# The state products of an S5 branch on unsplit float32 operands

## The chip, the cores and the metric

The kernel runs on one core of one Trainium2 chip. Five engines work side by side and meet only through semaphores: TensorE multiplies matrices (PE; its weight loads are listed as PEld), VectorE (DVE), ScalarE (ACT) and GpSimd (POOL) work on tiles in SBUF and PSUM, and SyncE (SP) issues nearly all DMAs. The metric is the device time of one execution in microseconds.

## The reference, cut to what matters

One layer of a hybrid encoder over 4096 tokens of width 1024: a norm, one combined projection, three branches side by side, an output projection, a second norm and the residual. The branch at issue is the state space model (SSM). Its 256 channels form 16 groups of 16 channels, each with 64 complex states per direction:

```python
bu = einsum('blgp,gnp->blgn', u, bb)                      # inputs into states (re, im)
h  = associative_scan(complex_linear_combine, lam, bu)    # forward and reverse
y  = einsum('blgn,gpn->blgp', h_re, c_re) - einsum('blgn,gpn->blgp', h_im, c_im)
```

The last line, the product of the states with C, is what is changed.

## The kernel before, in words

All products that need float32's precision are made from split parts: ScalarE rounds an operand to float32r (`hi`), VectorE or GpSimd subtracts that from the operand (`lo`), and TensorE makes three float32r products, hi·hi, hi·lo and lo·hi, into one PSUM bank (`mm3`, L989 to L992, is such a triple).

TensorE's order is written out by hand: `Slots` (L84) is a clock that advances by one slot after every 6 matmuls of the running projection (`chunk`, L354), and every helper step is booked into a slot with `e.at`. An engine's queue therefore holds its instructions in slot order, and waits stand in front of the instruction that needs them. The program has four stages: projections with weights and norm (stage 1), attention (stage 2), the gates' projections (stage 3, 24 slots for each of 8 blocks of 512 tokens, lines L1129 to L1155), and the output projection `w_out` (L1278).

The SSM runs inside stage 3, one group every 8 slots (`SSM_PACE`, L76), so three or four groups are under way at a time. A group's 512 columns hold 8 tokens each. Its steps, by the slot within the group (L1103 to L1109):

- 0: SP loads the group's record `rec` (weights, C, angles; 689 columns) and its inputs `u`.
- 3 to 7: splits of the record's input weights (`wb`) and of `u` (`ur`, its low part on POOL); the angles `ang` on POOL; ACT makes cosines and sines `cs` (slots 8 to 10).
- 11, 12: TensorE makes the inputs of the states, `vr` and `vi`, and the direct term, which opens the group's bank `y`.
- 12 to 14: DVE and POOL turn the inputs by the angles (tiles `wt` and `t`). Slot 14 also splits C into `wc` (L1064, L1065): ACT rounds it, DVE makes the low part one slot later.
- 15, 16: four DVE scans over half the partitions each (L1069, L1071) write `gs`.
- 18 to 23: the states are turned back: `back_cos` on DVE (wt<-gs,cs), `back_sin` on POOL (gs<-gs,cs), two sums on POOL (wt<-wt,gs).
- 25 to 27: the states are split into tiles `h`: ACT rounds, DVE makes two low parts (`state_lo`, L1088).
- 29, 30: six matmuls (y<-h,wc) add C times the states to `y`; 31: ACT copies `y` out; 33: SP stores it.

Of two groups' work in DVE's queue, the one that stands behind `back_cos` of a group is `state_lo` of the group before it, then the turning of the next. At the end of stage 3, `load_wo` (L1115) loads the output weights through three buffers (`rawo`), and DVE makes their low parts (`wo`).

Of the kernel before, what the change touches and what calls it, by code (L numbers as in the profile page):

```python
# [11 lines left out]
F32R = mybir.dt.float32r  # L12
# [4 lines left out]
P = 128  # L17
# [8 lines left out]
NC = SEQ // L  # L26
# [9 lines left out]
REC = 689  # L36
# [93 lines left out]
def hybrid_kernel(ctx, tc, A, out):  # L130
    nc = tc.nc
    V, S, PL, T = nc.vector, nc.scalar, nc.gpsimd, nc.tensor
    dma = nc.sync.dma_start
# [4 lines left out]
    swd = tc.dram_tile([G, P, REC], F32, name="swd")  # L138
# [22 lines left out]
    def tt(eng, out, in0, in1, op):  # L161
        return eng.tensor_tensor(out=out, in0=in0, in1=in1, op=op)  # L162
# [9 lines left out]
    def copy(out, in_):  # L172
        return S.activation(out=out, in_=in_, func=AF.Copy)  # L173

    def bank(i, shape, nm):
        return banks[i].tile(shape, F32, tag="b", name=nm)

    def bc(ap, shape):
        return ap.to_broadcast(shape)

    def f(ap):
        return ap.bitcast(F32)

    def lo_part(lo, src, hi, eng):
        tt(eng, lo, src, f(hi), ALU.subtract)

    def split(hi, lo, src, eng, lag=1, scale=None):

        copy(hi, src)
        if lag:  # L190
            e.at(e.now + lag, lo_part, lo, src, hi, eng)
        else:
            lo_part(lo, src, hi, eng)
# [795 lines left out]
    def mm3(o, wh, wl, r, first, last):  # L989
        T.matmul(o, lhsT=wh, rhs=r[:, 0], start=first, stop=False)  # L990
        T.matmul(o, lhsT=wh, rhs=r[:, 1], start=False, stop=False)
        T.matmul(o, lhsT=wl, rhs=r[:, 0], start=False, stop=last)  # L992

    def ssm_group(g, R, t0):


        sv = R["sv"]
        rho = bc(R["rho"][:, g:g + 1], [P, NC])
        X = {}

        def new(nm, shape, dt=F32, bufs=1):
            X[nm] = sv.tile(shape, dt, tag=nm, name=nm, bufs=bufs)
            return X[nm]

        def load():
            dma(out=new("rec", [P, REC], bufs=2), in_=swd[g])
            dma(out=new("u", [P, NC], bufs=2), in_=udram[g].rearrange("q s c -> s q c"))

        def inputs_hi():
            copy(new("ur", [P, 2, NC], F32R, 2)[:, 0], X["u"])  # L1010
            copy(new("wb", [P, 2, 3, P], F32R, 2)[:, 0], X["rec"][:, 0:384].rearrange("p (m c) -> p m c", m=3))

        def wb_lo():
            w = X["wb"]
            lo_part(w[:, 1], X["rec"][:, 0:384].rearrange("p (m c) -> p m c", m=3), w[:, 0], V)

        def turns():
            shc = [P, 16, 32]  # L1020
            rec = X["rec"]
            tt(PL, new("ang", shc), bc(rec[:, 672:688].unsqueeze(2), shc), bc(rec[:, 640:672].unsqueeze(1), shc),
               ALU.add)

        def ur_lo():
            lo_part(X["ur"][:, 1], X["u"], X["ur"][:, 0], PL)

        def angle_abs():
            cs = new("cs", [P, 2, NC], bufs=2)
            av = X["ang"].rearrange("p a b -> p (a b)")  # L1030
            S.activation(out=cs[:, 0], in_=av, func=AF.Abs)
            S.activation(out=cs[:, 1], in_=av, func=AF.Abs, bias=cst[:, C_NQ:C_NQ + 1])

        def angle_fold():
            S.activation(out=X["cs"], in_=X["cs"], func=AF.Abs, bias=cst[:, C_NHALF:C_NHALF + 1])

        def angle_sin():
            S.activation(out=X["cs"], in_=X["cs"], func=AF.Sin, scale=-TURN, bias=cst[:, C_HPI:C_HPI + 1])

        def inputs_mm():  # L1040
            w, ur = X["wb"], X["ur"]
            for i, nm in enumerate(("vr", "vi")):
                X[nm] = bank(4 + i, [P, NC], nm)
                mm3(X[nm], w[:, 0, i], w[:, 1, i], ur, True, True)

        def direct_mm():
            w = X["wb"]
            X["o"] = bank((6, 7, 2, 3)[g % 4], [P, NC], "y")
            mm3(X["o"], w[:, 0, 2], w[:, 1, 2], X["ur"], True, False)

        def turn_re():
            wt, t2 = new("wt", [P, 2, NC], bufs=2), new("t2", [P, 2, NC])
            tt(V, wt[:, 0], X["vr"], X["cs"][:, 0], ALU.mult)
            tt(V, t2[:, 0], X["vi"], X["cs"][:, 1], ALU.mult)

        def turn_im():
            wt, t2 = X["wt"], X["t2"]
            tt(PL, wt[:, 0], wt[:, 0], t2[:, 0], ALU.add)
            tt(V, wt[:, 1], X["vi"], X["cs"][:, 0], ALU.mult)
            tt(V, t2[:, 1], X["vr"], X["cs"][:, 1], ALU.mult)  # L1060

        def turn_sum():
            tt(PL, X["wt"][:, 1], X["wt"][:, 1], X["t2"][:, 1], ALU.subtract)
            wc = new("wc", [P, 2, 2, P], F32R, 2)  # L1064
            split(wc[:, 0], wc[:, 1], X["rec"][:, 384:640].rearrange("p (m c) -> p m c", m=2), V)  # L1065

        def scan(i):
            gs, wt = R["gs"][g % 2], X["wt"]
            V.tensor_tensor_scan(out=gs[0:64, i, 1:NC], data0=rho[0:64, 0:NC - 1], data1=wt[0:64, i, 0:NC - 1],  # L1069
                                 initial=0.0, op0=ALU.mult, op1=ALU.add)  # L1070
            V.tensor_tensor_scan(out=gs[64:128, i, NC - 2::-1], data0=rho[64:128, 0:NC - 1],  # L1071
                                 data1=wt[64:128, i, NC - 1:0:-1], initial=0.0, op0=ALU.mult, op1=ALU.add)

        sh2 = [P, 2, NC]

        def back_cos():
            tt(V, X["wt"], R["gs"][g % 2], bc(X["cs"][:, 0].unsqueeze(1), sh2), ALU.mult)

        def back_sin():
            tt(PL, R["gs"][g % 2], R["gs"][g % 2], bc(X["cs"][:, 1].unsqueeze(1), sh2), ALU.mult)  # L1080

        def back_sum(i):
            tt(PL, X["wt"][:, i], X["wt"][:, i], R["gs"][g % 2][:, 1 - i], ALU.add if i else ALU.subtract)

        def state_hi(i):
            copy(new(f"h{i}", [P, 2, NC], F32R)[:, 0], X["wt"][:, i])

        def state_lo():  # L1088
            for i in range(2):
                h = X[f"h{i}"]  # L1090
                lo_part(h[:, 1], X["wt"][:, i], h[:, 0], V)

        def state_mm(i):
            wc = X["wc"]
            mm3(X["o"], wc[:, 0, i], wc[:, 1, i], X[f"h{i}"], False, i == 1)

        def out_copy():
            copy(new("yg", [P, NC], bufs=2), X["o"])

        def store():  # L1100
            dma(out=ybuf[g].rearrange("q s c -> s q c"), in_=X["yg"])

        for t, fn, a in ((0, load, ()), (3, inputs_hi, ()), (4, wb_lo, ()), (6, turns, ()), (7, ur_lo, ()),  # L1103
                         (8, angle_abs, ()), (9, angle_fold, ()), (10, angle_sin, ()), (11, inputs_mm, ()),
                         (12, direct_mm, ()), (12, turn_re, ()), (13, turn_im, ()), (14, turn_sum, ()),
                         (15, scan, (0,)), (16, scan, (1,)), (18, back_cos, ()), (19, back_sin, ()),
                         (22, back_sum, (0,)), (23, back_sum, (1,)), (25, state_hi, (0,)), (26, state_hi, (1,)),
                         (27, state_lo, ()), (29, state_mm, (0,)), (30, state_mm, (1,)), (31, out_copy, ()),
                         (33, store, ())):  # L1109
            e.at(t0 + t, fn, *a, label="ssm")  # L1110

    WO = {}
# [284 lines left out]
    def to_p3():  # L1397
        e.settle("p2")
        R2["ph"].close()
        R3.update(p3_open())  # L1400
        for g in range(G):
            ssm_group(g, R3, e.now + int(SSM_PACE * g))
# [115 lines left out]
```

## Time and profile before

| | |
|---|---|
| median of three runs | 1667.59 us (1665.9 to 1668.29) |
| profiled execution | 1664.75 us, its span 1663.0 us |
| PE busy | 1574.8 us, 95% of the span |
| DVE busy | 1152.4 us, 69% |
| ACT busy | 766.5 us, 46% |
| POOL busy | 665.0 us, 40% |
| mean granted TensorE clock | 0.98 of full speed |
| SSM stretch | about 930 to 1250 us of the span |

Busy shares are averages over stages with different limits. A matmul's recorded length is that of one instruction in a pipeline, so neighbours overlap, and the distance from one start to the next is what a matmul costs. L162 is the line of a helper through which every two-operand instruction is recorded, so those are told apart by their tiles. A square bracket behind an instruction holds the engine's idle time ahead of it and what ended it.

### The profile page before, as it was taken

What the parts mean: (1) busy time and instruction counts of PE and PEld (TensorE: products, weight loads), DVE (VectorE), ACT (ScalarE), POOL (GpSimd) and SP (SyncE); (2) the same over time, 40 slices, a digit from 0 to 9 for tenths busy, and PEclk for the clock granted to TensorE, in tenths of its full rate; (3) what the DMA queues carried; (4) which work ended last, traced back from release to release, by engine and by line L of the source; (5) the groups of instructions that cost most, each with busy time, mean ns of one, the idle gap of its engine ahead of it and who ended that gap; (6) DMA issues with size and microseconds to landing.
All of it is one profiled execution on the core that took longest, in us unless ns stands there. A gap on an engine that the chain in (4) does not pass through costs nothing.

```text
span 1663.0 us, 20965 instructions
## 1 busy us (share of the span) xinstructions
PE 1574.8 (95%) x7364; PEld 1296.1 (78%) x7364; DVE 1152.4 (69%) x2047; ACT 766.5 (46%) x1624; POOL 665.0 (40%) x382
## 2 busy tenths in 40 slices
PE   8999899999999999999999989888879999999998
PEld 6787678888888888888888777676667788888886
DVE  5764676437777777777877399999985665555451
ACT  5424333346666666666776343433433333323221
POOL 0322122203233333233332277777752555555542
PEclk8999999999999999999999999999989999999999
DMA  6598999861111312123322655454635545555542
GB/s 227 174 301 262 285 302 309 290 237 63 64 64 64 118 66 71 64 75 116 133 89 89 209 182 169 121 176 144 207 122 183 188 156 176 176 179 179 176 152 76
DMA packets 131694, 267.60 MB, mean 161 GB/s; under 512 B 32386, under 2 KB 65922, under 8 KB 119812
## 3 DMA queue, kind: packets, MB, share of 16 engines
q1 hardware_dynamic: 126020, 251.57, 46.6%
q10 hardware_dynamic: 5568, 14.68, 2.6%
q8 instruction: 58, 0.95, 0.2%
q14 instruction: 48, 0.39, 0.1%
HBM read 173.25 MB, written 94.01 MB: 161 GB/s over the span
## 4 chain that ended last, share of the span: by engine, by line
PE 57%; DVE 22%; DMA 11%; issue 4%; POOL 4%; ACT 2%; SPq 1%; ACTq 0%; DVEq 0%; POOLq 0%
PE mm L350 7%; PE mm L351 7%; PE mm L352 7%; PE po L848 5%; DMA xs<-in_x_dram 5%; PE tp L858 5%; PE o L1289 5%; PE o L1287 5%; PE o L1288 5%; DVE gs L1069 4%; DVE gs L1071 4%; PE mm L361 4%; DVE h L162 3%; PE s L819 3%; PE s L818 3%
## 5 line engine op out<-in xcount | busy, mean ns | idle before, releaser
L350 PE MATMUL mm<-xk,w 128*128 128x512 f32 x968 | 388.3, 401 | 1.2 <-ACT xk L268 1.2
L351 PE MATMUL mm<-xk,w 128*128 128x512 f32 x968 | 383.5, 396 | 0.0
L352 PE MATMUL mm<-xk,w 128*128 128x512 f32 x968 | 382.1, 395 | 0.8 <-DVE w L162 0.8
L162 POOL TENSOR_TENSOR ns<-ns,es 128x1536 f32<-128x1536 f32 (+1 forms) x64 | 172.5, 2695 | 410.2 <-ACT pp L173 186.4
L352 PEld LDWEIGHTS mm<-xk,w 128*128 128x128 f32 x968 | 184.3, 190 | 41.9 <-DVE w L162 1.6
L350 PEld LDWEIGHTS mm<-xk,w 128*128 128x128 f32 x968 | 185.0, 191 | 36.6 <-ACT xk L268 1.9
L351 PEld LDWEIGHTS mm<-xk,w 128*128 128x128 f32 x968 | 184.7, 191 | 34.7 <-DVE xk L165 1.0
L820 DVE CUSTOM_DVE_ANT_0 ns<-s,cst,nsink 128x384 f32<-128x384 f32 (+1 forms) x256 | 145.7, 606 | 84.8 <-PE s L819 84.1
L1287 PE MATMUL o<-wo,yk 128*128 128x512 f32 x512 | 201.1, 393 | 3.0 <-ACT gg L1147 2.6
L1289 PE MATMUL o<-wo,yk 128*128 128x512 f32 x512 | 200.9, 392 | 2.1 <-DVE yk L165 2.1
L1288 PE MATMUL o<-wo,yk 128*128 128x512 f32 x512 | 200.4, 391 | 0.0
L173 ACT ACTIVATE pp<-tp 128x512 fp32r<-128x512 f32 x188 | 112.3, 597 | 170.6 <-PE tp L858 169.8
L361 PE MATMUL mm<-xk,w 128*128 128x512 f32 x552 | 149.3, 410 | 14.4 <-DVE xk L162 5.4
L809 ACT ACTIVATE ns<-ns,nm 128x384 f32<-128x384 f32 (+1 forms) x256 | 152.3, 598 | 2.0 <-DVE nm L820 2.0
L162 DVE TENSOR_TENSOR pp<-tp,pp 128x512 fp32r<-128x512 f32 x188 | 129.1, 687 | 18.8 <-ACT pp L173 17.4
L361 PEld LDWEIGHTS mm<-xk,w 128*128 128x128 f32 x552 | 103.3, 194 | 43.5 <-ACT xk L173 8.1
L848 PE MATMUL po<-pp,vr 128*128 128x512 f32 x376 | 127.8, 421 | 0.0
L162 POOL TENSOR_TENSOR xk<-xt,xk 128x512 fp32r<-128x512 f32 x32 | 51.8, 1625 | 172.8 <-ACT xk L173 111.0
L858 PEld LDWEIGHTS tp<-cst,ns 128*128 128x128 f32 x752 | 93.0, 140 | 34.6 <-issue 10.1
L858 PE MATMUL tp<-cst,ns 128*128 128x128 f32 x752 | 112.7, 272 | 7.3 <-DVE pp L162 7.3
L1287 PEld LDWEIGHTS o<-wo,yk 128*128 128x128 f32 x512 | 96.9, 189 | 24.4 <-ACT gg L1147 3.0
L1289 PEld LDWEIGHTS o<-wo,yk 128*128 128x128 f32 x512 | 96.9, 189 | 23.1 <-DVE yk L165 2.6
(293 smaller groups left out, 2795.3 us busy)
## 6 DMA issues: line engine op xcount, KB each, us to landing
xk<-xd SPq DMA_DIRECT2D x60, 1024.0 KB
xd<-xk SPq DMA_DIRECT2D x32, 1024.0 KB
xt<-in_xT_dram SPq DMA_DIRECT2D x35, 512.0 KB
xres<-in_x_dram SPq DMA_DIRECT2D x32, 512.0 KB
out_dram<-ot SPq DMA_DIRECT2D x31, 512.0 KB
xs<-in_x_dram ACTq DMA_DIRECT2D x24, 512.0 KB
raw<-in_w_in_dram SPq DMA_DIRECT2D x32, 256.0 KB
yattn<-ysb SPq DMA_DIRECT2D x32, 256.0 KB
```

The costliest lines, as they stand in the source:

```text
L162: return eng.tensor_tensor(out=out, in0=in0, in1=in1, op=op)
L350: T.matmul(o, lhsT=w[:, 0, k], rhs=xh, start=(k == 0), stop=False)
L351: T.matmul(o, lhsT=w[:, 0, k], rhs=xl, start=False, stop=False)
L352: T.matmul(o, lhsT=w[:, 1, k], rhs=xh, start=False, stop=(k == NK - 1))
L361: T.matmul(o, lhsT=w[:, i, k], rhs=XK[b, k][h], start=(n == 0), stop=(n == 3 * NK - 1))
L809: S.activation(out=ns[:, hh, :nk], in_=ns[:, hh, :nk], func=AF.Exp, scale=-1.0, bias=nm[:, hh:hh + 1], accum_out=su[:, hh:hh + 1])
L820: V.tensor_tensor_reduce(out=ns[:, hh, :nk], in0=sp_[:, :nk], in1=cst[:, C_D + c0:C_D + c0 + nk], scale=-(2.0 ** -(h + 1)), scalar=R["nsin ...
L848: T.matmul(po, lhsT=VR[:, (ta + kb) % 8, kv], rhs=pp[:, i], start=(kb == 0 and i == 0), stop=(kb == nkb - 1 and i == 1))
L858: T.transpose(tp[:, hh], ns[:, hh, kb * P:(kb + 1) * P], ident)
L1287: T.matmul(o, lhsT=y[:, 0, ts_], rhs=WO[kk][:, 0, hs], start=first, stop=False)
L1288: T.matmul(o, lhsT=y[:, 0, ts_], rhs=WO[kk][:, 1, hs], start=False, stop=False)
L1289: T.matmul(o, lhsT=y[:, 1, ts_], rhs=WO[kk][:, 0, hs], start=False, stop=last)
```

## The change

The six matmuls of a group's state products become two on float32 operands, straight from the record and from `wt`. The rounding and the low parts of `wc` and `h` go, with their tiles; the record, which is now read until the state products, gets four buffers instead of two; the products move from slots 29 and 30 to 26 and 27, the copy from 31 to 28 and the store from 33 to 30.

```diff
         def load():
-            dma(out=new("rec", [P, REC], bufs=2), in_=swd[g])
+            dma(out=new("rec", [P, REC], bufs=4), in_=swd[g])
             dma(out=new("u", [P, NC], bufs=2), in_=udram[g].rearrange("q s c -> s q c"))
...
         def turn_sum():
             tt(PL, X["wt"][:, 1], X["wt"][:, 1], X["t2"][:, 1], ALU.subtract)
-            wc = new("wc", [P, 2, 2, P], F32R, 2)
-            split(wc[:, 0], wc[:, 1], X["rec"][:, 384:640].rearrange("p (m c) -> p m c", m=2), V)
...
-        def state_hi(i):
-            copy(new(f"h{i}", [P, 2, NC], F32R)[:, 0], X["wt"][:, i])
-
-        def state_lo():
-            for i in range(2):
-                h = X[f"h{i}"]
-                lo_part(h[:, 1], X["wt"][:, i], h[:, 0], V)
-
         def state_mm(i):
-            wc = X["wc"]
-            mm3(X["o"], wc[:, 0, i], wc[:, 1, i], X[f"h{i}"], False, i == 1)
+            T.matmul(X["o"], lhsT=X["rec"][:, 384 + 128 * i:512 + 128 * i], rhs=X["wt"][:, i], start=False,
+                     stop=(i == 1))
...
-                         (22, back_sum, (0,)), (23, back_sum, (1,)), (25, state_hi, (0,)), (26, state_hi, (1,)),
-                         (27, state_lo, ()), (29, state_mm, (0,)), (30, state_mm, (1,)), (31, out_copy, ()),
-                         (33, store, ())):
+                         (22, back_sum, (0,)), (23, back_sum, (1,)), (26, state_mm, (0,)), (27, state_mm, (1,)),
+                         (28, out_copy, ()), (30, store, ())):
```

Lines behind the change have smaller numbers in the changed kernel: the scans L1069 and L1071 are L1067 and L1069 there, and the state products are L1084.

On VectorE, one group's round in the middle of the stretch, from one `back_cos` to the last scan ahead of the next, before:

```order
L162 TENSOR_TENSOR wt<-gs_8795,cs 128x1024
L162 TENSOR_TENSOR h_9226<-wt,h_9226 128x512
L162 TENSOR_TENSOR h_9237<-wt,h_9237 128x512
L162 TENSOR_TENSOR wt<-vr,cs 128x512
L162 TENSOR_TENSOR t_9275<-vi,cs 128x512
L162 TENSOR_TENSOR wb<-rec,wb 128x384
L162 TENSOR_TENSOR wt<-vi,cs 128x512
L162 TENSOR_TENSOR t_9275<-vr,cs 128x512
L1069 SCALAR_TENSOR_TENSOR gs_8798<-rho,wt 64x511
L1071 SCALAR_TENSOR_TENSOR gs_8798<-rho,wt 64x511
L162 TENSOR_TENSOR wc<-rec,wc 128x256
L1069 SCALAR_TENSOR_TENSOR gs_8798<-rho,wt 64x511
```

and in the changed kernel:

```order
L162 TENSOR_TENSOR wt<-gs_8795,cs 128x1024
L162 TENSOR_TENSOR wt<-vr,cs 128x512
L162 TENSOR_TENSOR t_9254<-vi,cs 128x512
L162 TENSOR_TENSOR wb<-rec,wb 128x384
L162 TENSOR_TENSOR wt<-vi,cs 128x512
L162 TENSOR_TENSOR t_9254<-vr,cs 128x512
L1067 SCALAR_TENSOR_TENSOR gs_8798<-rho,wt 64x511
L1069 SCALAR_TENSOR_TENSOR gs_8798<-rho,wt 64x511
L1067 SCALAR_TENSOR_TENSOR gs_8798<-rho,wt 64x511
L1069 SCALAR_TENSOR_TENSOR gs_8798<-rho,wt 64x511
```

Two `h` instructions and one `wc` instruction are gone, and the rest stands in the order it had. POOL's order is the same in both kernels.

On TensorE, where a block's first chunk (mm<-xk,w) meets a group's products, before:

```order
L361 MATMUL mm<-xk,w 128x512 x12
L990 MATMUL vr<-ur,wb 128x512
L991 MATMUL vr<-ur,wb 128x512
L992 MATMUL vr<-ur,wb 128x512
L990 MATMUL vi<-ur,wb 128x512
L991 MATMUL vi<-ur,wb 128x512
L992 MATMUL vi<-ur,wb 128x512
L361 MATMUL mm<-xk,w 128x512 x6
L990 MATMUL y<-ur,wb 128x512
L991 MATMUL y<-ur,wb 128x512
L992 MATMUL y<-ur,wb 128x512
L361 MATMUL mm<-xk,w 128x512 x6
```

and in the changed kernel:

```order
L361 MATMUL mm<-xk,w 128x512 x6
L1084 MATMUL y<-wt,rec 128x512
L361 MATMUL mm<-xk,w 128x512 x6
L1084 MATMUL y<-wt,rec 128x512
L990 MATMUL vr<-ur,wb 128x512
L991 MATMUL vr<-ur,wb 128x512
L992 MATMUL vr<-ur,wb 128x512
L990 MATMUL vi<-ur,wb 128x512
L991 MATMUL vi<-ur,wb 128x512
L992 MATMUL vi<-ur,wb 128x512
L361 MATMUL mm<-xk,w 128x512 x6
L990 MATMUL y<-ur,wb 128x512
```

The state products of a group now stand ahead of the `vr` of the group two after it; before, they stood a few slots behind that.

On VectorE at the end of the stretch, from the last group's `back_cos` on, before:

```order
L162 TENSOR_TENSOR wt<-gs_8798,cs 128x1024
L162 TENSOR_TENSOR h_10809<-wt,h_10809 128x512
L162 TENSOR_TENSOR h_10824<-wt,h_10824 128x512
L162 TENSOR_TENSOR wo<-rawo,wo 128x512
L162 TENSOR_TENSOR yk<-pgl,yk 128x1024
L162 TENSOR_TENSOR wo<-rawo,wo 128x512 x3
L162 TENSOR_TENSOR h_10914<-wt,h_10914 128x512
L162 TENSOR_TENSOR h_10925<-wt,h_10925 128x512
```

and in the changed kernel:

```order
L162 TENSOR_TENSOR wt<-gs_8798,cs 128x1024
L162 TENSOR_TENSOR wo<-rawo,wo 128x512
L162 TENSOR_TENSOR yk<-pgl,yk 128x1024
L162 TENSOR_TENSOR wo<-rawo,wo 128x512 x5
L162 TENSOR_TENSOR yk<-ya,yk 128x1024
```

The first low part of the output weights follows `back_cos` at once; before, two `h` instructions stood between them.

## Rows read from the trace of the kernel before

**Rows 1.** The page's first line.

```profile
span 1663.0 us, 20965 instructions
```

**Rows 2.** The chain of waits, one round: start us, us, what.

```profile
1045.17 3.40 DVE h L162 x2
...
1056.15 1.09 DVE wc L162
...
1061.66 1.23 DVE wt L162
```

**Rows 3.** Busy time by rounds: us, busy (instructions) by engine, clock, DMA, GB/s.

```profile
1007.45:1025.20 17.75, 17.48 (x64) 13.81 (x64) 17.52 (x14) 7.33 (x13) 13.21 (x7) 0.83 0.46 145
...
1096.02:1113.73 17.71, 14.71 (x63) 11.75 (x63) 17.48 (x14) 7.27 (x13) 13.17 (x7) 1.00 0.24 73
...
sum 230.31, PE 202.13 PEld 160.26 DVE 227.38 ACT 94.74 POOL 171.41; mean PE 15.55 PEld 12.33 DVE 17.49 ACT 7.29 POOL 13.19
```

**Rows 4.** Who waited for whom, 960 to 1203: total us, times, longest.

```profile
PE vr L991 <- POOL ur L162: 30.2, 14, 3.6
```

**Rows 5.** Timeline of DVE, the first rounds: start us, us, instruction.

```profile
957.81 1.22 DVE L162 TENSOR_TENSOR wt<-gs,cs 128x1024 f32<-128x1024 f32 x1
...
960.40 1.53 DVE L162 TENSOR_TENSOR wb<-rec,wb 128x384 fp32r<-128x384 f32 x1 [0.17 <-ACT wb L173]
...
967.60 1.10 DVE L162 TENSOR_TENSOR wc<-rec,wc 128x256 fp32r<-128x256 f32 x1
968.62 2.28 DVE L1069 TENSOR_TENSOR_SCAN gs<-rho,wt 64x511 f32<-64x511 f32 x1
...
973.09 1.23 DVE L162 TENSOR_TENSOR wt<-gs,cs 128x1024 f32<-128x1024 f32 x1
```

**Rows 6.** Timeline of POOL beside it.

```profile
959.11 2.41 POOL L162 TENSOR_TENSOR gs<-gs,cs 128x1024 f32<-128x1024 f32 x1 [4.25 <-DVE wt L162]
...
966.45 1.96 POOL L162 TENSOR_TENSOR ang<-rec 128x512 f32<-128x512 f32 x1
968.37 1.45 POOL L162 TENSOR_TENSOR wt<-wt,gs 128x512 f32<-128x512 f32 x1
969.78 2.19 POOL L162 TENSOR_TENSOR ur<-u,ur 128x512 fp32r<-128x512 f32 x1
```

**Rows 7.** Timeline of PE, one round at full clock.

```profile
1096.02 0.50 PE L991 MATMUL vr<-ur,wb 128*128 128x512 f32 x1 [1.44 <-POOL ur L162]
...
1110.33 0.40 PE L990 MATMUL vr<-ur,wb 128*128 128x512 f32 x1
1113.73 0.50 PE L991 MATMUL vr<-ur,wb 128*128 128x512 f32 x1 [3.00 <-POOL ur L162]
```

**Rows 8.** Float32 products of stage 1: all of a line, then two in the timeline.

```profile
L659 PE MATMUL kp<-obr,bz 128*64 128x128 f32 x32 | 6.9, 299 | 0.4 <-DVE obr L162 0.4
...
282.03 0.38 PE L659 MATMUL kp<-obr,bz 128*64 128x128 f32 x2
282.25 0.38 PE L661 MATMUL kp<-obi,bz 128*64 128x128 f32 x2
```

**Rows 9.** Timeline of DVE at the end of the stretch.

```profile
1205.22 4.34 DVE L162 TENSOR_TENSOR h<-wt,h 128x512 fp32r<-128x512 f32 x2
...
1222.03 1.33 DVE L162 TENSOR_TENSOR wc<-rec,wc 128x256 fp32r<-128x256 f32 x1
1223.28 1.21 DVE L1069 TENSOR_TENSOR_SCAN gs<-rho,wt 64x511 f32<-64x511 f32 x1
...
1228.95 3.47 DVE L162 TENSOR_TENSOR h<-wt,h 128x512 fp32r<-128x512 f32 x2
1232.35 1.77 DVE L162 TENSOR_TENSOR wo<-rawo,wo 128x512 fp32r<-128x512 f32 x1
```

**Rows 10.** Timeline of PE, its two longest pauses after that.

```profile
1229.69 0.80 PE L991 MATMUL y<-h,wc 128*128 128x512 f32 x1 [9.57 <-DVE h L162]
...
1254.79 0.50 PE L1287 MATMUL o<-wo,yk 128*128 128x512 f32 x1 [2.57 <-ACT gg L1147]
```

## The prediction, on record before the changed kernel was run

> **What bounds the kernel now.** I read the chain of waits first. From 960 to 1203 us it holds hardly anything but VectorE: scans, the two low parts of `h` (3.40 us), the low part of `wc` (1.09 us), then `back_cos` (wt<-gs,cs) of the next group, and round again [rows 2]. The table of rounds comes next. Between one `vr` wait and the next lie 17.71 to 17.75 us, 13 rounds take 230.31 us, so 17.72 us each, and DVE is busy for 17.49 of them: it is the bound [rows 3]. TensorE is not. In a round at full clock it has 14.71 us of work [rows 3] and then stands still until POOL has made the low part of `ur`: 3.00 us in the round shown, 30.2 us in 14 waits [rows 4, 7]. So TensorE follows this stretch at DVE's pace, although it is 95% busy over the span, and what shortens DVE's round shortens the program down to the next limit.
>
> **What goes.** From DVE, per group, the pair of `h` and `wc`. Start to start, `wc` takes 968.62 - 967.60 = 1.02 us [rows 5], and the pair is 3.40 us of the chain [rows 2]: 4.4 us of 17.72. From ACT go three copies per group; it is busy for 7.29 us of a round [rows 3], so that counts for nothing.
>
> **What the round comes down to.** DVE's own sum would be 17.7 - 4.4 = 13.3 us. POOL stands in the way: `back_cos` is followed by `back_sin` (gs<-gs,cs) on POOL, POOL then makes the sums that the scans wait for, and DVE and POOL slow each other. `wb` lasts 1.53 us and ends at 961.93, just after `back_sin` has ended at 959.11 + 2.41 = 961.52 [rows 5, 6]. The trace holds one round that already lacks the pair: the low parts of the first group stand behind `back_cos` at 973.09, so the round from `back_cos` at 957.81 to that at 973.09 has none [rows 5]. It takes 15.28 us, and only `wc` is in it that the changed kernel lacks. How much of that goes? At least the time in which `wc` alone runs: POOL's `ang` ends at 966.45 + 1.96 = 968.41 and `wc` at 967.60 + 1.10 = 968.70, so 0.29 us; POOL's instructions from 966.45 to 969.78 + 2.19 = 971.97 stand end to end and stay [rows 5, 6]. At most its 1.02 us. The new round is thus 14.3 to 15.0 us. I take 15.0, since POOL's row of instructions does not get shorter by `wc`'s going.
>
> This is where a rule of the Trainium skill speaks against a larger gain: "SBUF — State Buffer", section "Who interferes with whom", has VectorE (with two SBUF inputs) and GpSimd take one shared port pair as an exclusive lock, for a whole instruction, with the other fully blocked. By it the two engines' instructions add up instead of overlapping, and the gap that `wc` leaves is filled by the next of POOL's: 15.0 rather than 14.3. The `wb` that ends 0.41 us behind `back_sin` agrees.
>
> **What TensorE needs.** From 1096.02 to 1110.33, and 0.23 for the last, 14.54 us hold 63 matmuls [rows 3, 7]: 0.231 us each. Six go: 57 x 0.231 = 13.15 us. Two float32 products of 512 columns come, and no row shows one. The nearest: 16 float32 products of 128 columns (L659, four for each of four batches) have 32 records, so a product is two, and two products start 282.25 - 282.03 = 0.22 us apart [rows 8]. Four times the columns can take four times as long at most, 0.88 us; at least two matmuls' pace, 0.46 us. TensorE's round is then 13.15 + 2 x 0.46 = 14.1 to 13.15 + 2 x 0.88 = 14.9 us. The three products that one replaces took 0.69, so TensorE may gain or lose. I take 0.88, since streaming 512 columns is what these rows scale with, and 14.9 is still under 15.0: its cover is thin, 0.1 us of each round.
>
> "FP8 and Floating Point Precision", section "TensorE Precision Notes", in the Trainium skill has true float32 take four passes. By it a product would be 4 x 0.231 = 0.92 us, the round 15.0, and the cover nothing.
>
> **Waits that are added.** The products now wait for POOL's sums themselves, where ACT and DVE stood between, and behind them in TensorE's queue stand `vr` and all of the projection. But the second sum ends at 969.82, and `ur`, for which `vr` waits anyway, at 971.97 [rows 6]: 2.15 us later, while product and first `vr` take 0.88 + 0.23. So no new pause. The record's next load waited for `wc`; with four buffers it waits for state products of four groups earlier, long past. POOL's queue is unchanged, SP's store comes earlier.
>
> **Before and after these rounds.** Group 0's `wc` stands alone on DVE ahead of 957.81: 1.0 us. The round 957.81 to 973.09 gives 15.28 - 15.0 = 0.3. At the end, between the last rounds and the first low part of the output weights (`wo`, 1232.35), go a pair of 4.34 us, a `wc` of 1223.28 - 1222.03 = 1.25 us and a pair of 1232.35 - 1228.95 = 3.40 us [rows 9]. POOL's instructions fill part of the pairs' place, so 1.25 to 9.0 us; I take the middle, 5. Loads of output weights wait for `wo`'s buffers, and on them `w_out` at 1254.79. TensorE gets there in time: its pause of 9.57 us for `h` goes or shrinks [rows 10], and its pause ahead of `w_out` stays. All behind that is as before.
>
> **Sum.** 13 x (17.72 - 15.0) = 35.4, and 1.0 + 0.3 + 5 = 6.3: 41.7 us. The profiled execution took 1664.75 us (span 1663.0 [rows 1]); less 41.7 that is 1623. The median of the runs shown is 2.8 us above the profiled one, so 1626 us.
>
> **Rivals.**
>
> 1. DVE and POOL overlap more than I grant; the round is 14.3, with TensorE's products near 0.46. 13 x 3.42 = 44.5, 1.0 + 1.0, and 9 at the end: 55 us, so 1612. For it: bounds from rows, above. Against it: `wb`'s wait.
>
> 2. TensorE becomes the bound through its clock. In the round from 1007.45 the granted clock is 0.83 of 2.4 GHz, so part of it at 1.2 GHz, after a wait for `ur`, and TensorE's work is 17.48 instead of 14.71 us [rows 3]. In 13 rounds TensorE is busy for 202.13 us, 13 x 14.71 = 191.2 at full clock, so 10.9 us went to the lower level, hidden in TensorE's pauses. If that stays, a round needs 14.9 + 0.84 = 15.7: 13 x 2.0 + 6.3 = 32 us, so 1635. Against it: such a drop stands behind pauses of TensorE, and those nearly vanish.
>
> 3. A product of 512 columns costs more than four of 128, 1.7 us say (each record twice my upper value). Round 13.15 + 3.4 = 16.6: 13 x 1.1 + 6.3 = 21, so 1646. For it: no row of that shape. Against it: rows 8.
>
> 4. The stretch keeps its pace: something beside DVE holds it at 17.7, as a load that arrives late. Only the end's 1 to 5 us go: 1664. Against it: DVE is busy for all but 0.2 us of a round [rows 3].
>
> 5. Slower: the lower clock takes hold of the stretch. TensorE needs 14.9 us a round at full clock, so it exceeds today's 17.72 once the mean clock is below 14.9 / 17.72 = 0.84. At 0.75 a round is 19.9 us: 13 x 2.2 - 6 = 22 more, so 1690. For it: 0.83 has been seen in one round. Against it: in that round TensorE had waited for POOL, and here it is to be busy throughout.
>
> **How the numbers follow.** Forecast 60% (its own range 1617 to 1634), rival 1 12%, rival 2 13%, rival 3 7%, rival 4 4%, rival 5 4%. The range 1610 to 1642 takes in the first two rivals and leaves out the others, some 15%. No change within 0.2% (3.3 us, about what a measurement of this kernel tells from none) is rival 4; faster is the rest but rival 5: 92%, 4%, 4%.
>
> **What would show it.** Right: in the rounds, `back_cos` to `back_cos` of 15.0 us; DVE idle for about a microsecond per round at the scans, waiting for POOL; POOL with hardly an idle stretch; four PE records per group on L1084, starting some 0.44 us apart; the `vr` wait under half a microsecond and the clock at 1.00; `wo` and `w_out` some 42 us earlier. Wrong: rounds of 15.5 us or more with PE without a pause (product or clock); rounds of 14.5 or less; a pause on L1084 itself for POOL's sums; or rounds at 15 and `w_out` less than 35 us earlier, which would mean that a load at the stretch's end takes the gain back.

## The result and the profile after

The changed kernel takes 1623.91 us (median of four runs, 1621.85 to 1628.71), the kernel before on the same chip 1666.74 us (four runs, 1664.34 to 1668.29). The ratio is 0.9746, with a 95% interval of 0.9723 to 0.9769. The profiled execution of the changed kernel, 1628.71 us, is the slowest of its four, and that of before, 1664.75 us, is 2.0 us under its median; the two profiles therefore show a difference of 36.0 us where the medians show 42.8.

The first line of the page answers to [rows 1]:

```profile
span 1626.8 us, 20824 instructions
```

The table by windows answers to [rows 3]. Its columns are the stretch, its length, the busy time (instructions) of PE, PEld, DVE, ACT and POOL, the granted clock, the DMA share and GB/s. The rows are the first round (from `back_cos` to `back_cos`) and the thirteen behind it:

```profile
960.74:974.63 13.89, 13.28 (x55) 9.89 (x54) 13.82 (x11) 5.33 (x9) 12.59 (x7) 1.00 0.70 234
974.63:1167.21 192.58, 191.79 (x792) 147.64 (x791) 185.71 (x130) 79.06 (x118) 176.99 (x92) 1.00 0.59 193
```

192.58 / 13 = 14.81 us a round, where it was 17.72. TensorE is now busy for all but 0.79 us of the thirteen rounds, and its clock is at 1.00. The waits in this stretch answer to [rows 4]; the columns are total us, number and longest:

```profile
PE vr L991 <- POOL ur L162: 0.8, 1, 0.8
...
POOL gs L162 <- DVE wt L162: 15.1, 13, 1.2
```

TensorE's wait for the low part of `ur` has all but gone: 0.8 us in place of 30.2. The wait that remains is POOL's, 1.16 us in each round, until DVE has finished `back_cos`.

One round of DVE (its four products out of PSUM left out), and then POOL beside it, answer to [rows 5, 6]. The columns are start, us, instruction and, in brackets, idle time before it with what ended it:

```profile
1137.64 2.12 DVE L162 TENSOR_TENSOR wt<-gs,cs 128x1024 f32<-128x1024 f32 x1
...
1140.89 1.78 DVE L162 TENSOR_TENSOR wb<-rec,wb 128x384 fp32r<-128x384 f32 x1
...
1143.87 2.29 DVE L1067 TENSOR_TENSOR_SCAN gs<-rho,wt 64x511 f32<-64x511 f32 x1
1146.17 2.16 DVE L1069 TENSOR_TENSOR_SCAN gs<-rho,wt 64x511 f32<-64x511 f32 x1
1148.34 1.91 DVE L1067 TENSOR_TENSOR_SCAN gs<-rho,wt 64x511 f32<-64x511 f32 x1
1150.26 2.15 DVE L1069 TENSOR_TENSOR_SCAN gs<-rho,wt 64x511 f32<-64x511 f32 x1
1152.44 2.12 DVE L162 TENSOR_TENSOR wt<-gs,cs 128x1024 f32<-128x1024 f32 x1
```

```profile
1136.49 2.19 POOL L162 TENSOR_TENSOR ur<-u,ur 128x512 fp32r<-128x512 f32 x1
1139.84 2.41 POOL L162 TENSOR_TENSOR gs<-gs,cs 128x1024 f32<-128x1024 f32 x1 [1.16 <-DVE wt L162]
1142.20 1.63 POOL L162 TENSOR_TENSOR wt<-wt,t 128x512 f32<-128x512 f32 x1
1143.79 1.29 POOL L162 TENSOR_TENSOR wt<-wt,gs 128x512 f32<-128x512 f32 x1
1145.04 2.20 POOL L162 TENSOR_TENSOR wt<-wt,t 128x512 f32<-128x512 f32 x1
1147.21 1.96 POOL L162 TENSOR_TENSOR ang<-rec 128x512 f32<-128x512 f32 x1
1149.13 2.19 POOL L162 TENSOR_TENSOR wt<-wt,gs 128x512 f32<-128x512 f32 x1
1151.29 2.19 POOL L162 TENSOR_TENSOR ur<-u,ur 128x512 fp32r<-128x512 f32 x1
```

In this round DVE shows no idle time, but it does wait. `back_cos`, 1.22 us in [rows 5], now lasts 2.12: POOL's `ur` ends at 1138.68, a microsecond into it. `back_cos` then ends at 1139.76, and POOL's `back_sin` begins at 1139.84. A wait between these two engines stands inside the duration of the instruction that waits, on POOL too: its sums of 128x512 last 1.29 to 2.20 us in this one round. POOL's records stand end to end but for one idle stretch: 13.61 us busy and 1.16 us of waiting make the round.

Read by their ends, these lines are one row. After `back_cos` (1139.76) end `back_sin` at 1142.25 and `wb` at 1142.67; then two sums of POOL, then scan, sum, scan, `ang`, scan, sum, scan, `ur` and `back_cos`, each 0.84 to 1.25 us behind the end before it, although their records are up to 2.29 us long. The last end is 1154.56, and the whole row is 14.80 us: the round.

The float32 products on TensorE, in its timeline, have two records each (x2):

```profile
1031.66 1.02 PE L1084 MATMUL y<-wt,rec 128*128 128x512 f32 x2
1032.12 1.95 PE L361 MATMUL mm<-xk,w 128*128 128x512 f32 x6
1033.90 1.02 PE L1084 MATMUL y<-wt,rec 128*128 128x512 f32 x2
```

From one product to the next are 2.24 us, which hold one product and six matmuls at about 0.227 us (the pace of the projection's matmuls from 1039.70 to 1045.83). 2.24 - 1.36 = 0.88 us for a product of 512 columns, 0.44 a record.

Place by place, in the two profiles:

| stretch | before, us | after, us | difference | predicted |
|---|---|---|---|---|
| start of the program to start of the SSM stage | 930.04 | 932.84 | +2.8 | 0 |
| from there to the `back_cos` that opens the first round | 27.77 | 27.90 | +0.1 | -1.0 |
| first round | 15.28 | 13.89 | -1.4 | -0.3 |
| the next 13 rounds | 230.29 | 192.58 | -37.7 | -35.4 |
| last `back_cos` to first low part of `wo` | 28.97 | 25.41 | -3.6 | -5 |
| `wo` to `w_out` | 22.44 | 24.00 | +1.6 | 0 |
| `w_out` to the end | 408.21 | 410.18 | +2.0 | 0 |
| sum | 1663.0 | 1626.8 | -36.2 | -41.7 |

The places are starts of instructions: the SSM stage starts with DVE's first instruction in it, and `w_out` stands for the matmul of L1276 (L1287 in before) ahead of which PE pauses, as in [rows 10]; the first matmul of that line starts at 1251.38 before and 1210.70 after. The first and the last row hold no changed code, and the stage's start lies between 927.81 and 935.58 us in the runs below; the rows between give 41.0 us. At the end of the stretch PE paused for `h`, 9.57 us [rows 10], and now pauses 2.86 us for POOL's sums. Within `w_out` it pauses longer, 5.08 us where it was 2.57:

```profile
1182.84 1.12 PE L1084 MATMUL y<-wt,rec 128*128 128x512 f32 x2 [2.86 <-POOL wt L162]
...
1216.62 0.79 PE L1276 MATMUL o<-wo,yk 128*128 128x512 f32 x1 [5.08 <-ACT gg L1136]
```

The chain behind this pause can be followed one step further. In ACT's queue `gg` stands behind a rounding that waits for POOL's product with the gates (`ya`), and that product waits for a DMA of the gates (`ga`, `agate`), first in before and then after:

```profile
1250.79 2.37 POOL L162 TENSOR_TENSOR ya<-ya,ga 128x1024 f32<-128x1024 f32 x1 [7.33 <-DMA agate<-gg]
```

```profile
1212.65 2.34 POOL L162 TENSOR_TENSOR ya<-ya,ga 128x1024 f32<-128x1024 f32 x1 [10.34 <-DMA ga<-agate]
```

The load of `ga` is issued at 1244.93 in before and at 1204.56 after, so POOL's product starts 5.86 us behind the issue in before and 8.09 after.

### The profile page after: what moved, and what is told of

Read it like the earlier page. It is cut to its first block, busy times and chain, and to the rows that moved or that the text cites. A ratio compares the mean times of both kernels' runs of the same rounds, so it can differ in the third digit from the quotient of the medians.

```text
span 1626.8 us, 20824 instructions
## 1 busy us (share of the span) xinstructions
PE 1570.2 (97%) x7332; PEld 1285.3 (79%) x7332; DVE 1110.9 (68%) x1999; ACT 746.6 (46%) x1576; POOL 673.2 (41%) x382
## 4 chain that ended last, share of the span: by engine, by line
PE 61%; DMA 14%; DVE 11%; POOL 6%; issue 5%; SPq 2%; ACT 2%; ACTq 0%; POOLq 0%; DVEq 0%
PE mm L350 8%; PE mm L351 8%; PE mm L352 8%; PE po L848 5%; DMA xs<-in_x_dram 5%; PE tp L858 5%; PE mm L361 4%; PE o L1276 4%; PE o L1278 4%; PE o L1277 4%; PE s L819 3%; PE s L818 3%; DMA xt<-in_xT_dram 2%; POOL ot L162 2%; DMA ga<-agate 1%
## 5 line engine op out<-in xcount | busy, mean ns | idle before, releaser
L1276 PE MATMUL o<-wo,yk 128*128 128x512 f32 x512 | 201.5, 394 | 5.5 <-ACT gg L1136 5.1
L1276 PEld LDWEIGHTS o<-wo,yk 128*128 128x128 f32 x512 | 97.0, 189 | 27.0 <-ACT gg L1136 5.5
```

Source lines behind the costliest of these rows:

```text
L1276: T.matmul(o, lhsT=y[:, 0, ts_], rhs=WO[kk][:, 0, hs], start=first, stop=False)
```

## The experiments

The theory behind the prediction (A in the expectations below): DVE's and POOL's mutually excluding instructions make the round, and TensorE's own need lies just under it. Its main rival (B): with hardly a pause left, TensorE alone sets the round. The third (C): DVE and POOL alone, with TensorE far below. In what follows a round is the mean over the same thirteen, and ratios are to the kernel before.

### One state product less on TensorE

The product with the imaginary half is left out:

```diff
-            T.matmul(X["o"], lhsT=X["rec"][:, 384 + 128 * i:512 + 128 * i], rhs=X["wt"][:, i], start=False,
-                     stop=(i == 1))
+            if i == 0:
+                T.matmul(X["o"], lhsT=X["rec"][:, 384:512], rhs=X["wt"][:, 0], start=False, stop=True)
```

> The changed kernel without the second of a group's two state products (the imaginary half is left out of y), so TensorE's round is shorter by one float32 product, 0.88 us: 14.8 to 13.9. Instructions of DVE and POOL are as in the changed kernel. Theory A (two limits of equal height: the row of DVE and POOL instructions that exclude each other, 14.8 us, and TensorE's own work, 14.8): the round stays at 14.7 to 14.8, TensorE pauses about 0.9 us per round for ur, and the time stays within 3 us of the changed kernel's 1624. Theory B (TensorE alone sets the round, DVE and POOL have slack): round 13.9 to 14.0, some 11 us faster, 1613. Theory C (DVE and POOL alone): as A.

Measured: 1621.37 us, 0.9716 (0.9692 to 0.974). The rounds by windows, and then the wait of TensorE:

```profile
973.37:1165.96 192.59, 183.73 (x766) 143.03 (x767) 186.54 (x130) 79.08 (x118) 177.12 (x92) 1.00 0.59 194
```

```profile
PE vr L991 <- POOL ur L162: 10.3, 13, 2.5
```

The round stays at 14.81 us, and the time freed on TensorE (191.79 to 183.73 us of work) comes back as a wait for POOL's `ur`, in every round. TensorE alone doesn't set the round, though it is 99.6% busy: B falls.

### One instruction less on POOL

The low part of `ur` is not computed, and the matmuls read the high part in its place, as many as before:

```diff
+    def mm3h(o, wh, wl, r, first, last):
+        T.matmul(o, lhsT=wh, rhs=r[:, 0], start=first, stop=False)
+        T.matmul(o, lhsT=wh, rhs=r[:, 0], start=False, stop=False)
+        T.matmul(o, lhsT=wl, rhs=r[:, 0], start=False, stop=last)
...
-            mm3(X["o"], w[:, 0, 2], w[:, 1, 2], X["ur"], True, False)
+            mm3h(X["o"], w[:, 0, 2], w[:, 1, 2], X["ur"], True, False)
...
-        for t, fn, a in ((0, load, ()), (3, inputs_hi, ()), (4, wb_lo, ()), (6, turns, ()), (7, ur_lo, ()),
+        for t, fn, a in ((0, load, ()), (3, inputs_hi, ()), (4, wb_lo, ()), (6, turns, ()),
```

> The changed kernel without POOL's low part of ur (the three products that read it read the high part instead, so TensorE has the same number of matmuls). The row of DVE and POOL loses about 1.07 us: 14.8 to 13.7. Theory A: TensorE holds the round at 14.8, time within 3 us of 1624. Theory B: the same, 14.8. Theory C (DVE and POOL alone set the round, TensorE has slack): round 13.7, some 14 us faster, 1610.

Measured: 1618.24 us, 0.9696 (0.9669 to 0.9724).

```profile
970.99:1161.05 190.06, 190.06 (x789) 147.86 (x788) 167.67 (x130) 79.50 (x118) 148.99 (x79) 1.00 0.60 194
```

```profile
971.30 0.80 PE L995 MATMUL vr<-ur,wb 128*128 128x512 f32 x1
...
1162.84 0.79 PE L995 MATMUL vr<-ur,wb 128*128 128x512 f32 x1
```

An instruction whose record was 2.19 us long is gone, and the round, as a mean over DVE's thirteen, shortens by 0.19 only, to 14.62 us. TensorE is busy for 190.06 of 190.06 us and now sets the pace: from one group's first `vr` to that of the thirteenth group after it are 191.54 us, 14.73 a round. That is what TensorE needs, 0.08 us under the 14.81 of the changed kernel. DVE runs ahead in rounds of 13.96 to 14.11 us, waits for `vr` in eleven places (14.1 us in all), and has rounds of up to 16.17. C expected 13.7 throughout and falls. The time is 5.7 us under the changed kernel's, more than the 3 us that A allowed; the rounds hold 2.5 of that, and the rest was not followed up.

### Both at once

> Both of the edits at once: no second state product, no low part of ur (both are left out of the computation). Theory A: only now does the round fall, to 13.7 to 14.0 us, by 13 x 0.9 = 11 us or so: 1612. Theory B: as its forecast for the kernel without the second product, 13.9 to 14.0, no more gained by ur. Theory C: 13.7, as its forecast for the kernel without ur's low part.

Measured: 1611.26 us, 0.9655 (0.9632 to 0.9679).

```profile
969.13:1150.82 181.69, 181.39 (x769) 143.81 (x767) 176.59 (x131) 78.75 (x118) 150.48 (x79) 1.00 0.64 207
```

13.98 us a round: less work on POOL or on TensorE alone gives 0.19 us and nothing, on both 0.83. This is what two limits of nearly equal height do. The rounds are 13.96 to 13.99 us each, as those of the run before in which DVE ran ahead, and DVE waits for `vr` in none of them. So 13.97 is the row of DVE and POOL without the low part of `ur`. TensorE, with 14.73 - 0.88 = 13.85 us to do by these runs, lies 0.1 under it; its busy time of 181.39 of 181.69 us doesn't show that small gap.

### `ang` twice on POOL

```diff
+            tt(PL, X["ang"], bc(rec[:, 672:688].unsqueeze(2), shc), bc(rec[:, 640:672].unsqueeze(1), shc),
+               ALU.add)
```

> The changed kernel with POOL's instruction ang made twice per group (same operands, same result), so POOL has one more instruction of two SBUF operands; alone it takes 0.84 to 1.05 us. Theory A and C (DVE's and POOL's instructions exclude each other, so each one lengthens the row): the round grows by 0.8 to 1.1 us to 15.6 to 15.9, 11 to 14 us slower, 1637. Theory B (TensorE alone, with slack in DVE and POOL, or the two overlapping): 14.8 and 1624 as before.

Measured: 1635.76 us, 0.9799 (0.9773 to 0.9824). The windows, and POOL's timeline in one round:

```profile
974.06:1178.21 204.15, 194.21 (x788) 146.92 (x788) 173.07 (x130) 79.05 (x118) 201.07 (x105) 1.00 0.56 181
```

```profile
1063.91 3.88 POOL L162 TENSOR_TENSOR ang<-rec 128x512 f32<-128x512 f32 x2
```

The round grows by 0.89 us, to 15.70, while TensorE's work stays at 194.21 of 204.15 us. One of the thirteen is 16.91 us long, and the other twelve are 15.60 in the mean, 0.79 more. ACT waits 2.9 us for a load of `u` in the long one; such waits stand in rounds of the usual length too, so why it is long stays open. The pair of `ang` is recorded 1.92 us longer than the single one (1.96 us), but that holds waiting: the first group's `ang`, at 937.93 in the changed kernel, lasts 1.05 us. So the round grew by a little less than what one `ang` takes by itself. DVE's busy time falls from 185.71 to 173.07 us with the same 130 instructions, so part of what it had been was not work. Work added to POOL lengthens the round. POOL's work alone doesn't set it: at the shortest records of their shapes its eight instructions a round (2.4, four of 1.3, two of 1.05 and 1.27) would take 11 us. So the row that POOL shares with DVE is the limit.

### An operation of DVE out of PSUM twice

```diff
             tt(V, t2[:, 1], X["vr"], X["cs"][:, 1], ALU.mult)
+            tt(V, t2[:, 1], X["vr"], X["cs"][:, 1], ALU.mult)
```

> The changed kernel with one of DVE's four products out of PSUM (t<-vr,cs) made twice per group: 0.6 us more of DVE's time, of the kind that did not slow beside POOL in the trace. Theory (only instructions with two SBUF operands exclude POOL's, and they set the round): the round stays under 15.1, the time within 4 us of 1624. Rival (DVE's own sum of times sets the round): 0.6 us more per round, 15.4, 8 us slower.

Measured: 1628.24 us, 0.9775 (0.9757 to 0.9792).

```profile
971.52:1164.65 193.13, 191.71 (x792) 147.59 (x791) 187.16 (x144) 79.15 (x118) 177.20 (x92) 1.00 0.59 194
```

```profile
1066.64 1.40 DVE L162 TENSOR_TENSOR t<-vr,cs 128x512 f32<-128x512 f32 x2
1067.96 1.64 DVE L1068 TENSOR_TENSOR_SCAN gs<-rho,wt 64x511 f32<-64x511 f32 x1
```

The round is 14.86 us in the mean: 14.79 to 14.81 in twelve of the thirteen, as before, and 15.61 in one, which again has a wait for a load of `u` (2.7 us on ACT). DVE does about 0.7 us more, and the scan behind it, 2.29 us long in the changed kernel, lasts 1.64: it begins later and ends no later. DVE's own sum therefore does not set the round, although its records cover 96% of it. A DVE instruction that takes one input from PSUM runs beside POOL (0.67 to 0.69 us in all 64 records of the changed kernel), and what the added one took was waiting time. The time is 4.3 us over 1624, just outside the 4 us of the theory; the rounds hold 0.6 of that.

### Before, without the pair of `h` only

The low parts of `h` are left out, and four matmuls remain of the six:

```diff
-            mm3(X["o"], wc[:, 0, i], wc[:, 1, i], X[f"h{i}"], False, i == 1)
+            h = X[f"h{i}"]
+            T.matmul(X["o"], lhsT=wc[:, 0, i], rhs=h[:, 0], start=False, stop=False)
+            T.matmul(X["o"], lhsT=wc[:, 1, i], rhs=h[:, 0], start=False, stop=(i == 1))
...
-                         (27, state_lo, ()), (29, state_mm, (0,)), (30, state_mm, (1,)), (31, out_copy, ()),
+                         (29, state_mm, (0,)), (30, state_mm, (1,)), (31, out_copy, ()),
```

> The kernel before without the two low parts of h on DVE (the product with them is left out, so four state matmuls per group instead of six); the low part of wc stays, the slots stay. If the pair was what DVE's round paid for: the round falls from 17.72 to the 15.2 or so of the trace's one round without the pair, 13 x 2.5 = 32 us, and with the end of the stretch 36 us: 1631. If instead the rounding on ACT, the record's buffers or the earlier slots brought the gain, the time stays near 1667.

Measured: 1632.83 us (1624.48 to 1639.55), 0.9813 (0.9773 to 0.9853).

```profile
971.98:1171.42 199.44, 186.12 (x789) 148.37 (x788) 195.82 (x144) 94.31 (x156) 168.99 (x92) 0.99 0.58 194
```

A round is 15.34 us, so the pair is worth 17.71 - 15.34 = 2.37 us, close to the 17.72 - 15.28 = 2.44 that the prediction read from the one round without it. The pair is 3.40 us long [rows 2], so a microsecond of its place is filled otherwise when it goes.

### Before, without the low part of `wc` only

Here too the products with it go, and four matmuls remain of the six:

```diff
-            split(wc[:, 0], wc[:, 1], X["rec"][:, 384:640].rearrange("p (m c) -> p m c", m=2), V)
+            copy(wc[:, 0], X["rec"][:, 384:640].rearrange("p (m c) -> p m c", m=2))
...
-            mm3(X["o"], wc[:, 0, i], wc[:, 1, i], X[f"h{i}"], False, i == 1)
+            h = X[f"h{i}"]
+            T.matmul(X["o"], lhsT=wc[:, 0, i], rhs=h[:, 0], start=False, stop=False)
+            T.matmul(X["o"], lhsT=wc[:, 0, i], rhs=h[:, 1], start=False, stop=(i == 1))
```

> The kernel before without the low part of wc on DVE (the product with it is left out, four state matmuls per group instead of six); the pair of h stays. If DVE's and POOL's instructions exclude each other and only the time in which wc alone ran goes, the round falls by 0.3 us to 17.4, 4 us in all, 1662; if all of its 1.02 us go, to 16.7, 13 to 15 us, 1652.

Measured: 1658.93 us, 0.9968 (0.9956 to 0.998).

```profile
972.90:1196.34 223.44, 193.02 (x793) 153.57 (x793) 220.73 (x157) 93.69 (x158) 180.82 (x92) 0.96 0.50 168
```

17.19 us a round: `wc` is worth 0.52, between the 0.29 and the 1.02 of the prediction. 2.37 + 0.52 = 2.89 us, and the whole change brought 17.71 - 14.81 = 2.90 a round. The two removals add up, and what else the change does comes to nothing in sum; that its single parts do nothing isn't shown, and the slots, below, do much.

### Before, with the record in three buffers

```diff
-            dma(out=new("rec", [P, REC], bufs=2), in_=swd[g])
+            dma(out=new("rec", [P, REC], bufs=3), in_=swd[g])
```

> The kernel before with three buffers for the record instead of two (four don't fit beside h and wc), so that a record's load no longer waits for the low part of wc of the group two ahead, for which the DMA queue stood still for 137 us in all. Theory (DVE's round bounds): no change, within 3 us of 1667. Rival (the waiting DMA queue held the stretch up, and the record's buffers brought part of the gain): faster by 5 us or more.

Measured: 1665.99 us, 1.0006 (0.9992 to 1.002).

```profile
977.69:1207.78 230.09, 199.38 (x821) 158.33 (x820) 227.18 (x169) 93.07 (x156) 172.24 (x92) 0.96 0.50 164
```

A round of 17.70 us. SP's wait for `wc` ahead of the record's load, 126.3 us in thirteen waits in before, is gone, and so an earlier load of the record brings nothing by itself. In the changed kernel the product reads the record itself, and so holds its buffer longer; what fewer than four would cost there was not tried.

### The products in their old slots

The changed kernel with products, output copy and store at the slots of before:

```diff
-                         (22, back_sum, (0,)), (23, back_sum, (1,)), (26, state_mm, (0,)), (27, state_mm, (1,)),
-                         (28, out_copy, ()), (30, store, ())):
+                         (22, back_sum, (0,)), (23, back_sum, (1,)), (29, state_mm, (0,)), (30, state_mm, (1,)),
+                         (31, out_copy, ()), (33, store, ())):
```

> The changed kernel with the products back in slots 29 and 30, the copy in 31 and the store in 33. Theory (work per round decides, not the place): within 3 us of 1624, the round at 14.8. Rival (the earlier place spares TensorE a wait or costs it one): rounds that differ by 0.3 us or more, 4 us in the time.

Measured: 1728.05 us, 1.0385 (1.0362 to 1.0408), slower than before the change. No expectation came near it. The windows, the wait that leads, and DVE's timeline at one such wait:

```profile
968.61:1263.94 295.33, 221.88 (x793) 167.67 (x793) 175.96 (x131) 79.96 (x118) 174.82 (x92) 0.88 0.38 128
```

```profile
DVE wt L162 <- PE y L1084: 118.4, 13, 9.8
```

```profile
1047.63 0.69 DVE L162 TENSOR_TENSOR wt<-vr,cs 128x512 f32<-128x512 f32 x1 [9.30 <-PE y L1084]
```

The round is 22.72 us. DVE's first product out of `vr` (`turn_re`) stands still for 9 us in each round until TensorE has done the state products of two groups earlier. The reason, read from the code and tested in the next run: `wt` has two buffers, and in before the copies to `h` were its last readers. Now the state products read `wt` themselves, so that `turn_re` of the group two ahead, which writes the same buffer and is issued in slot 28 of this group, must wait for them. In slots 26 and 27 they stand ahead of that; in 29 and 30 they stand in TensorE's queue behind that group's `vr`, `vi` and direct term and the projection between, while DVE waits. TensorE waits in turn, 71.1 us for `ur` in thirteen waits, and its granted clock falls to 0.88 in the mean, so for a part of the time it is at the lower of its two levels, 1.2 GHz.

### The old slots, with a third buffer for `wt`

This is the test of that reading, with the slots of the run before:

```diff
-            wt, t2 = new("wt", [P, 2, NC], bufs=2), new("t2", [P, 2, NC])
+            wt, t2 = new("wt", [P, 2, NC], bufs=3), new("t2", [P, 2, NC])
```

> The changed kernel with its products in the old, late slots (29 and 30, copy 31, store 33) and three buffers for wt instead of two. New theory on the late slots' loss (rounds of 22.72 us): the products now read wt themselves, wt's second buffer is written by the turning of the group two ahead in slot 28, so DVE has to wait for a product that stands behind in TensorE's queue. Then a third buffer gives the round back: 14.8 us, 1624. Rival (the late place itself costs it, by the order of TensorE's queue or of ACT's copy and SP's store): rounds stay above 20 us, 1700 and more.

Measured: 1627.43 us, 0.9769 (0.9753 to 0.9785).

```profile
973.00:1167.36 194.36, 193.28 (x788) 148.55 (x789) 184.27 (x131) 80.69 (x118) 176.97 (x92) 0.99 0.57 190
```

14.95 us a round in place of 22.72; one round is 16.43, with a wait for a load of `u` (5.3 us on ACT), and the others are 14.76 to 14.91. The buffer was the cause, and either the earlier slots or a third buffer avoids it.

### A fourth buffer for the raw weights

`w_out` now waits 5.08 us for the gate's product (`gg`) where it waited 2.57. One more buffer for the raw weights was to bring what stands before it forward:

```diff
-    wraw = ctx.enter_context(tc.tile_pool(name="wraw", bufs=3))
+    wraw = ctx.enter_context(tc.tile_pool(name="wraw", bufs=4))
```

> The changed kernel with four buffers instead of three for the raw weights, so that one more load of output weights goes out before the first low part of wo frees a buffer, and the gate loads queued behind (ga) go out earlier; w_out's first matmul waited 5.1 us at the end of that chain. If that chain of loads is what w_out waits for: 2 to 5 us faster than the changed kernel, 1619 to 1622. If the loads merely collide elsewhere: no change, 1624.

Measured: 1622.85 us, 0.9739 (0.972 to 0.9757).

```profile
1218.26 0.79 PE L1276 MATMUL o<-wo,yk 128*128 128x512 f32 x1 [5.21 <-ACT gg L1136]
```

The pause stays at 5.21 us and the round at 14.81, and the interval holds the changed kernel's own 0.9746. A fourth of these buffers doesn't shorten the pause. The load of `ga` is issued at 1206.73 here, 5.49 us ahead of the first matmul of `w_out` (1212.22), where it was 6.14 us ahead in the changed kernel, so it didn't come earlier for `w_out`. Why POOL's product starts 8.09 us behind the issue in the changed kernel and 5.86 in before stays open.

## Why the prediction came out right

**What bounds the round.** It said that DVE's and POOL's instructions, which exclude each other, make the row that sets the round, with TensorE thinly under it. That is what the runs show: more on POOL lengthens the round by 0.89, more on DVE out of PSUM by 0.05 only, less on TensorE changes nothing. The row of ends, 14.80 us, shows the same in the trace itself. The rule cited from the Trainium skill, "SBUF — State Buffer", section "Who interferes with whom", agrees with these numbers.

**The size of the round.** 14.81 us instead of 15.0. The pair was sized right, 2.44 forecast and 2.37 measured. The term that was off is `wc`: the sentence "I take 15.0, since POOL's row of instructions does not get shorter by `wc`'s going" granted 0.29 us, the lower of two bounds, and it is worth 0.52. So its going shortens the row by more than the part in which it ran alone. The rows show most of the rest: in [rows 5, 6] `back_cos` begins at 973.09, when `ur` has long ended (971.97), and takes its whole 1.23 us; in the changed kernel it is issued while `ur` runs and ends 1.08 us behind it. 0.23 us more for `wc` and 0.07 less for the pair are 13 x 0.16 = 2.1 of the 2.3 us by which the thirteen rounds gained more than forecast.

**TensorE.** The float32 product measures 0.88 us, the upper bound that was taken. That the cost would grow with the columns was assumed, since no row of before showed it; it held. The estimate of 0.92 from the Trainium skill, "FP8 and Floating Point Precision", section "TensorE Precision Notes", is 0.04 above the measured 0.88. The work of a round was forecast as 14.9 us, and the run without POOL's low part of `ur` shows 14.73. The cover is 0.08 us, close to the 0.1 of the forecast, with both limits some 0.2 lower. The clock stayed at 1.00, with no pauses of TensorE left in these rounds but one of 0.8 us. The clock speaks against rivals 2 and 5; rivals 1 and 3 needed rounds of 14.3 and 16.6 us, and rival 4 needed unchanged ones.

**Added waits.** "So no new pause" held in the rounds, but it was argued from POOL's sums and `ur` only. That the product now holds `wt`'s buffer was not seen, and it is the largest effect in all these runs: with the products in their old slots and two buffers, the change makes the kernel 3.85% slower than before. The prediction read the move as a matter of TensorE's waits; its main use is to free `wt` in time.

**Before and after the rounds.** Ahead of the first round nothing was gained (+0.1 against -1.0). The length of this piece hangs on more than DVE: `vr` came 1.4 us later in the stage than in before, and the piece is 26.93 to 28.22 us in four other runs with the changed code there (one product less, the late slots, the third buffer for `wt`, four raw buffers). The first round gave 1.4 instead of 0.3. Of that, 0.9 lies only in where the round is marked off, since the `back_cos` that ends it is recorded 2.12 us long in place of 1.23; from end to end the round went from 15.29 to 14.79, by 0.50, close to the 0.52 of `wc`; the run without `wc`'s low part alone has 13.91 and 14.80. That both pieces together give 1.3 in forecast and measurement is chance. The end gave 3.6 us against 5, inside its bounds of 1.25 to 9. "Its pause ahead of `w_out` stays" was wrong: the pause grew by 2.5 us, from 2.57 to 5.08, and the piece from `wo` to there by 1.6.

**The marks.** Two were wrong in form. DVE was to be idle for a microsecond per round at the scans: it waits, but within its instructions. POOL was to have hardly an idle stretch: it has one, 1.16 us, ahead of `back_sin`. The wait at `vr` was to stay under half a microsecond: it is 0.8 us in the first of the thirteen rounds and none in the others. The other marks came as said: two records a product, some 0.44 us each, and `wo` 39.7 and `w_out` 38.2 us earlier, or 42.5 and 41.0 counted from the stage's start, which came 2.8 us later in this execution.

## What to carry to other kernels

Where DVE instructions with two SBUF inputs alternate with POOL's, add the two engines' instructions up along one row, from end to end rather than by their recorded lengths, and bound a removed instruction's gain by the part that runs alone and by its whole length. Don't trust the busy share: a DVE at 96% had slack, and a TensorE at 99.6% was not the bound. When a consumer is moved from a copy to the original tile, look up who writes that buffer next and whether the consumer stands ahead of that writer in its own queue; a slot or a third buffer decided 8 us of a round of 15 here.

## What the runs showed of the hardware that was not expected

- Waiting between DVE and POOL shows as longer instructions, not as idle time: `back_cos` 1.22 us in before and 2.12 after, with the same shape; POOL's `ang` 1.05 us for the first group and 1.96 in the rounds. The scan's 2.29 us fell to 1.64 when it began later. A duration next to POOL's work is thus no price of the operation.
- A float32 matmul of 128x512 is two records, 0.88 us in all at full clock, against about 0.227 us of a matmul of the same shape on split operands: 3.9 times one, and 1.3 times the three that it replaces. It takes more of TensorE and still pays here, since the splitting was on the engines that bound the round.
